# An inner Strassen level, in place, for a second product of the output stage

## The chip, the cores and the metric

The kernel runs on one core of a Trainium2 chip. The metric is device time in microseconds (us) of that core for one execution. Median before: 909.28 us over 3 runs (909.12 to 909.48).

## The reference, cut to what matters

The depth is 1, so that only the pooling mixer runs: a norm of the rows, an input product of 1024 x 2048, trailing means over windows of 2, 4, 8 and 16 rows in four channel groups, a map for each group, a gate, an output product of 1024 x 1024, the residual, and a last norm of the rows.

```
h = x                                            # 4096 x 1024, float32
u, gate = split(rms_norm(h, norm_w) @ in_w, 2)
pooled  = trailing_mean(u per group, window) - u
y       = (pooled @ group_w + group_b) * scale * silu(gate)
h       = h + y @ out_w
out     = rms_norm(h, final_norm_w)
```

## The kernel before, in words

**Stages.** `steps` lists the work in order: stage "a" and stage "b" (each half of the channel groups, 4 blocks of 1024 rows, with the group maps folded into the input weights), then stage "o", the output product, 8 blocks b of 512 rows (`NBO`, `TO`). Every block's product is done by the Strassen-Winograd scheme: seven products P1 to P7 of half-size operands, in stage "o" in the order of `ORDER_OUT`: P1, P7, P6, P2, P5, P4, P3.

**Float32 by three passes.** An operand is kept as a high part (a copy that is rounded, on ScalarE) and a low part (operand minus high part, on VectorE); `split` makes both, in one of four tiles `op0` to `op3` that are used in turn (`next_op`). A product adds high x high, high x low and low x high (`mm3`). A product of stage "o" is 2 row groups j x 4 k x 3 passes, that is 24 matmuls of 128 columns of weights against 512.

**Banks.** PSUM has 8 banks, in pairs. `sets_of` gives each block of stage "o" a pair x (P1, then P2 on top), a pair v (P7, then P4 on top), a pair y (P1 copied in by ScalarE, then P6, P5 and P3 on top) and a spare pair; the next block turns the roles by three pairs, so that the old spare pair is the new x, the old x the new v, and the old v the new y. `evict_o` takes each product from its pair: P7, P6 and P2 are copied by ScalarE into rows `hs[b]` in SBUF (and `add_h` has GpSimd issue transfers that add x to them), P5, P4 and P3 are added to these rows by VectorE (line 1245). A row is done after P4 (the lower half of the block, half 1) or P3 (the upper half, half 0); `finish` then takes the sum of squares on ScalarE (line 1121, the squares themselves thrown into a free SBUF tile), works out 1/rms in `inverse` with a square root on ScalarE and small steps on VectorE and GpSimd, scales the rows on VectorE (line 1125) and stores them by SP.

**Inner products.** From block 2 on, P2 is itself done by seven inner products ("leaves") of quarter-size operands (`split_inner`, `product_inner`, line 879): 7 x 2 k x 3 passes, that is 42 matmuls against 256 columns. Their results lie in x and in the spare pair and are put together by adds on VectorE (`add_inner`, line 889). The inner weights of P2 are formed during block 1 (`load_inner`, `form_inner`) and lie in four tiles that are taken out of the pool for good (`kept`). In stage "b", blocks 1 and 2, product P7 is done by 14 leaves in place (`product_seven`, line 725): the results move between the halves of one bank pair by copies on ScalarE (`move`), later leaves add on top, and one add on VectorE ends it.

**What sets the order.** The functions issue the instructions; a scheduler orders each engine's queue at build time, held by the explicit `issue_after` edges, and each engine works its queue strictly in that order. `advance` runs ahead of the products: loads by 4 steps, splits by 2. `split_o` forms the operands of stage "o" (s3 = s11 - s21 for P7, and so on) from four loaded quarters of y, s11, s12, s21 and s22. Tiles come from two pools, `st` (11) and `vt` (8); `take` gives the one that has been free the longest, and a load into it waits for that tile's last reader or transfer. All loads and stores of this stage wait in SP's one queue.

Of the kernel before, what the change touches and what calls it, by code (L numbers as in the profile page):

```python
# [25 lines left out]
HIST = 16  # L26
NS = 11
NV = 8
EPS = 1e-6

P1, P2, P3, P4, P5, P6, P7 = range(1, 8)
# [33 lines left out]
def kernel(  # L65
# [739 lines left out]

    inner, inner_w, kept = {}, {}, []
# [5 lines left out]
    def load_inner():  # L814
        inner_w["raw"] = [take() for _ in range(2)]
        for h, u in enumerate(inner_w["raw"]):
            nc.sync.dma_start(out=u, in_=wod[P2][h])

    def form_inner(stage):

        pattern, sizes = "p (n k s a) -> p n k s a", dict(n=2, k=2, s=2)
        if stage == 0:
            us = inner_w.pop("raw")
            b11, b12 = (quarter(us[0], j) for j in range(2))
            b21, b22 = (quarter(us[1], j) for j in range(2))
            raw = inner_w["sums"] = [take(pattern, **sizes) for _ in range(2)]
            (t3, t2), (t1, t4) = ([r[:, n] for n in range(2)] for r in raw)
            sub(t3, b22, b12)
            add(t2, t3, b11)
            sub(t1, b22, t2)  # L830
            sub(t4, b21, t2)
            for u in us:
                give(u)
            return
        r = inner_w["sums"][stage - 1]
        hi, lo = (
            kept.pop().rearrange("p x (y s a) -> p x y s a", y=2, s=2) for _ in range(2)
        )
        copy(hi, r)
        sub(lo, r, hi.bitcast(F32))  # L840
        give(r)
        for n, i in enumerate(((P7, P6), (P5, P4))[stage - 1]):
            inner_w[i] = [v[:, n] for v in (hi, lo)]
        for i, (h, j) in {P1: (0, 0), P2: (1, 0), P3: (1, 1)}.items():
            inner_w[i] = [quarter(w[P2][h][:, s], j) for s in range(2)]

    def split_inner(u):

        at = u.rearrange("p (g k) (j c) -> p g j k c", g=2, j=2)
        a11, a21, a12, a22 = (at[:, g, j] for g in range(2) for j in range(2))  # L850
        v = take("p (n k c) -> p n k c", n=4, k=2)
        sub(v[:, 0], a11, a21)
        sub(v[:, 1], a22, v[:, 0])
        add(v[:, 2], v[:, 1], a11)
        sub(v[:, 3], a12, v[:, 1])
        ts = [
            next_op("p (s g k j c) -> p s g j k c", s=2, g=2, k=2, j=2),
            next_op("p (s n k c) -> p s n k c", s=2, n=4, k=2),
        ]
        split(ts[0].rearrange("p s g j k c -> p s (g k) (j c)"), u)  # L860
        split(ts[1], v)
        give(v)
        t = {P1: ts[0][:, :, 0, 0], P2: ts[0][:, :, 1, 0], P4: ts[0][:, :, 1, 1]}
        t.update({i: ts[1][:, :, n] for n, i in enumerate((P7, P6, P5, P3))})
        return t

    def product_inner(i):

        t, sets = inner["t"], inner["sets"]
# [4 lines left out]
        for k in range(2):  # L874
            a = [t[i][:, s, k] for s in range(2)]
            b = [inner_w[i][s][:, k].rearrange("p s a -> p a s") for s in range(2)]
            ps = bank.rearrange("p (a s) -> p a s", s=2)[:, half * P : (half + 1) * P]
            for n, (x1, x2) in enumerate(((a[0], b[0]), (a[0], b[1]), (a[1], b[0]))):
                latest[0] = nc.tensor.matmul(  # L879
                    ps, x1, x2, start=i in (P1, P7) and k + n == 0, stop=k == 1 and n == 2,  # L880
                    skip_group_check=True,
                ).ins

    def add_inner(bank, *places):

# [5 lines left out]
    def sets_bank(n):  # L891
        return inner["sets"]["spare"][n]

    def product_out(i, t, sets, last):
        ps = sets[bank_of[i]]
        if isinstance(t, dict):
            inner.update(t=t, sets=sets)
            for p in (P2, P3, P4, P1, P7):
                product_inner(p)
            return  # L900
        for j in range(2):
            if j == 1 and inner and i == P5:
                product_inner(P6)
                add_inner(0, (1, 0))
                add_inner(1, (1, 0), (1, 1))
            rows = slice(j * P, (j + 1) * P)
            size = H // 4 if last and j == 1 else H // 2
            for c in range(0, H // 2, size):
                dst = sets["spare"][0] if c else ps[j]
                for k in range(4):  # L910
                    wk = w[i][k // 2]
                    mm3(
                        dst,
                        (t[:, 0, k, rows], t[:, 1, k, rows]),
                        (wk[:, 0, k % 2], wk[:, 1, k % 2]),
                        (i in (P1, P7) or c > 0) and k == 0,
                        k == 3,
                        slice(c, c + size),
                    )

# [147 lines left out]
    def load_o(b, i):  # L1068
        s = oxs[b]
        if i == P1:  # L1070
            s["11"] = load_y(b, 0, 0)
        elif i == P7:
            s["21"] = load_y(b, 1, 0)
        elif i == P6:
            s["22"] = load_y(b, 1, 1)
        elif i == P2:
            s["12"] = load_y(b, 0, 1)
            load_h(b, 1)
        elif i == P5:
            load_h(b, 0)  # L1080

    def split_o(b, i):
        s = oxs[b]
        if i == P2 and b > 1:
            return split_inner(s["12"])
        t = next_op("p (s a b) -> p s a b", s=2, a=4)
        if i == P7:
            s["3"] = take("p (a b) -> p a b", a=4)
            sub(s["3"], s["11"], s["21"])
        elif i == P6:  # L1090
# [22 lines left out]
        r = b * TO + (1 - half) * TH + j * P  # L1113
        return slice(r, r + P)

    def finish(b, half):
        ss = small.tile([P, 2], F32, tag="ss", name=f"oss{b}_{half}")
        us = [hs[b].pop((half, j)) for j in range(2)]
        for j in range(2):
            junk = take("p (a b) -> p a b", a=2)  # L1120
            nc.scalar.activation(junk, us[j], AF.Square, accum_out=ss[:, j : j + 1])
            give(junk)
        rs = inverse(b, half, ss)
        for j in range(2):
            nc.vector.scalar_tensor_tensor(  # L1125
                out=us[j], in0=us[j], scalar=rs[:, j : j + 1], in1=fw[0],
                op0=ALU.mult, op1=ALU.mult,
            )
            nc.sync.dma_start(
                out=out[row_of(b, half, j), :], in_=us[j].rearrange("p a b -> p (a b)")  # L1130
            )
            give(us[j])
# [81 lines left out]
    def evict_o(b, i, sets):  # L1214
# [64 lines left out]
        if final and i == P5:  # L1279
            for j in range(2):  # L1280
                early_half(half, j, n)
        elif not final and i in (P4, P3):
            finish(b, 1 if i == P4 else 0)

# [37 lines left out]
    def run(n, between=None, behind=None, seeds=4):  # L1322
        kind, b, i = steps[n]
        sets = sets_of(kind, b)
        if kind == "o":
            product_out(i, split_up.pop(n), sets, n == len(steps) - 1)
            evict_o(b, i, sets)
        else:
# [231 lines left out]
        )  # L1560

    scales, summed = {}, []
    stages = (P6, P5, P4)
    forming_seven = (P7, P6, P5, P4)

    for n in range(2, len(steps)):
# [4 lines left out]
        if ahead:  # L1571
# [12 lines left out]
        if kind == "o" and b == 1 and len(kept) < 4 and not inner_w:  # L1584
            while len(kept) < 4 and len(st.free) > 2:
                kept.append(st.keep())
            if len(kept) == 4:
                load_inner()
        elif kept:
            keep[0] = 0  # L1590
        advance("split", n, split_step, split_reach)
        if kind == "o" and b == 1 and i in stages:
            with tc.issue_after(latest_split[0]), tc.issue_after(latest_copy[0]):
                form_inner(stages.index(i))
# [105 lines left out]
```

## Time and profile before

| | |
|---|---|
| median of 3 runs | 909.28 us |
| profiled execution | 909.13 us, span 907.3 us, granted clock 0.997 |
| PE busy | 898.9 us (99%) |
| PEld busy | 790.2 us (87%) |
| DVE busy | 731.5 us (81%) |
| ACT busy | 494.0 us (54%) |
| POOL busy | 83.9 us (9%) |

PE is TensorE with its matmuls, PEld its weight loads, DVE VectorE, ACT ScalarE, POOL GpSimd, and SP the queue that issues most transfers. The page has the busy time of each engine, the chain of work that ended last, the costliest groups of instructions, and the transfers. The other views used here are the timeline (start, length, engine, line, what was written from what, and in square brackets how long the engine had been idle and who ended it), groups of instructions by shape (busy time, mean ns of one), busy time by stretches, waits, and transfers with the time from issue to landing. Lengths on one engine overlap a little: the next instruction can start some 0.08 us before the end of the one before. Matmul ends are modelled.

### The profile page before, as it was taken

The numbers are of one execution on the slowest core, as the hardware profiler recorded it, in microseconds if no ns is written. First come the engines' busy times: TensorE is split into PE (matmuls) and PEld (weight loads), VectorE is DVE, ScalarE is ACT, GpSimd is POOL, SyncE is SP. The second block draws the span as 40 slices with busy tenths as digits, with TensorE's granted clock in tenths as the row PEclk, the third lists the DMA queues.
The fourth block names the chain that finished last, engine by engine and source line by source line (L and its number), as shares of the span: only waits on it lengthen the run. The fifth ranks groups of instructions, "written<-read, shape, count | busy, mean of one in ns | idle before, by whom it ended". The sixth has DMA issues, their size and how long they took to land.

```text
span 907.3 us, 11824 instructions
## 1 busy us (share of the span) xinstructions
PE 898.9 (99%) x4392; PEld 790.2 (87%) x4392; DVE 731.5 (81%) x868; ACT 494.0 (54%) x760; POOL 83.9 (9%) x166
## 2 busy tenths in 40 slices
PE   9999999999999999999999999999999999999996
PEld 7888888888888888889889888888888898988986
DVE  3889896985995999798599499599759768868686
ACT  7869547447446565346545636545535435445434
POOL 0020100100110000000000000001122113112200
PEclk9999999999999999999999999999999999999998
DMA  9987667677575462323554475528585675775732
GB/s 341 401 303 238 251 229 229 215 270 251 224 267 198 161 217 85 110 100 116 206 189 148 176 267 168 192 70 232 173 232 172 171 192 158 169 220 162 175 140 92
DMA packets 71401, 179.41 MB, mean 198 GB/s; under 512 B 6576, under 2 KB 24624, under 8 KB 71344
## 3 DMA queue, kind: packets, MB, share of 16 engines
q1 hardware_dynamic: 58720, 146.13, 46.4%
q0 software_dynamic: 11904, 31.48, 13.5%
q10 hardware_dynamic: 720, 1.06, 0.3%
q8 instruction: 34, 0.56, 0.3%
q14 instruction: 23, 0.19, 0.1%
HBM read 117.81 MB, written 60.83 MB: 197 GB/s over the span
## 4 chain that ended last, share of the span: by engine, by line
PE 95%; DVE 2%; DMA 1%; ACT 1%; issue 0%; DVEq 0%; ACTq 0%
PE bank L779 89%; PE bank L879 3%; PE bank L725 2%; PE bank L421 1%; DMA st<-in_x 1%; DMA early<-in_wut 0%; ACT st L461 0%; DVE vt L1245 0%; ACT st L1152 0%; PE bank L487 0%; DVE vt L172 0%; DVE w L169 0%; ACT st L443 0%; ACT early L443 0%; DVE vt L1204 0%
## 5 line engine op out<-in xcount | busy, mean ns | idle before, releaser
L779 PE MATMUL bank<-op,w 128*128 128x512 f32 x2592 | 560.9, 379 | 0.0
L779 PEld LDWEIGHTS bank<-op,w 128*128 128x128 f32 x2592 | 489.4, 189 | 70.2 <-ACT vt L175 0.4
L779 PE MATMUL bank<-w,op 128*128 128x512 f32 (+1 forms) x1212 | 262.2, 377 | 0.0
L779 PEld LDWEIGHTS bank<-w,op 128*128 128x128 f32 x1212 | 226.0, 189 | 31.0
L169 DVE TENSOR_TENSOR op<-st,op 128x1024 fp32r<-128x1024 f32 x134 | 162.3, 1219 | 58.0 <-ACT op L175 57.6
L175 ACT ACTIVATE op<-st 128x1024 fp32r<-128x1024 f32 x134 | 140.2, 1052 | 113.4 <-PE bank L779 64.5
L175 ACT ACTIVATE vt<-bank 128x512 f32<-128x512 f32 (+1 forms) x115 | 65.8, 590 | 46.5 <-PE bank L779 43.1
L169 DVE TENSOR_TENSOR st<-st,st 128x1024 f32<-128x1024 f32 (+1 forms) x42 | 45.8, 1104 | 18.9 <-ACT st L256 16.8
L169 DVE TENSOR_TENSOR op<-vt,op 128x1024 fp32r<-128x1024 f32 x42 | 51.1, 1219 | 8.1 <-ACT op L175 8.1
L175 ACT ACTIVATE op<-vt 128x1024 fp32r<-128x1024 f32 x42 | 44.1, 1054 | 24.9 <-PE bank L779 20.9
L1062 POOL DMA_DIRECT2D st<-in_x x19 | 16.8, 893 | 387.0 <-DVE op L169 352.9
L175 ACT ACTIVATE st<-bank 128x512 f32<-128x512 f32 (+1 forms) x61 | 34.7, 585 | 30.6 <-PE bank L779 19.1
L175 ACT ACTIVATE bank<-bank 128x512 f32<-128x512 f32 (+1 forms) x60 | 32.1, 537 | 30.1 <-PE bank L779 26.0
L933 DVE TENSOR_TENSOR_SCAN vt<-vt,window 128x1040 f32<-128x1040 f32 x16 | 37.9, 2376 | 1.6 <-DMA yd<-vt 1.5
L169 DVE TENSOR_TENSOR w<-st,w 128x1024 fp32r<-128x1024 f32 (+1 forms) x26 | 30.8, 1198 | 9.2 <-ACT w L175 9.2
L175 ACT ACTIVATE w<-st 128x1024 fp32r<-128x1024 f32 (+1 forms) x26 | 26.6, 1035 | 17.4 <-PE bank L779 9.5
L175 ACT ACTIVATE vt<-tails 128x32 f32<-128x32 f32 x28 | 6.3, 228 | 46.8 <-DVE vt L933 25.7
L979 DVE SCALAR_TENSOR_TENSOR vt<-vt,vt 128x1024 f32<-128x1024 f32 x24 | 29.3, 1219 | 0.3
L172 DVE TENSOR_TENSOR st<-st,vt 128x1024 f32<-128x1024 f32 x22 | 26.1, 1215 | 3.4 <-DMA vt<-rd 3.4
L1125 DVE SCALAR_TENSOR_TENSOR vt<-vt,ors,st 128x1024 f32<-128x1024 f32 x18 | 22.5, 1282 | 7.6 <-POOL ors L235 7.6
L1245 DVE TENSOR_TENSOR st<-bank,st 128x512 f32<-128x512 f32 x23 | 15.8, 689 | 14.0 <-PE bank L779 14.0
L984 DVE SCALAR_TENSOR_TENSOR st<-vt,colt,st 128x512 f32<-128x512 f32 x38 | 26.8, 743 | 0.1
(143 smaller groups left out, 735.3 us busy)
## 6 DMA issues: line engine op xcount, KB each, us to landing
st<-in_xt SPq DMA_DIRECT2D x28, 512.0 KB, 6.3
sd<-st POOLq DMA_DIRECT2D x28, 512.0 KB, 4.0
st<-sd SPq DMA_DIRECT2D x26, 512.0 KB, 4.2
st<-in_x SPq DMA_DIRECT2D x20, 512.0 KB, 6.0
st<-yd SPq DMA_DIRECT2D x20, 512.0 KB, 4.6
yd<-st SPq DMA_DIRECT2D x19, 512.0 KB, 3.1
out<-vt SPq DMA_DIRECT2D x18, 512.0 KB, 4.6
st<-wod SPq DMA_DIRECT2D x15, 512.0 KB, 4.0
```

What stands on the lines that cost most here:

```text
L169: return nc.vector.tensor_tensor(out=dst, in0=a, in1=b, op=ALU.subtract)
L172: nc.vector.tensor_tensor(out=dst, in0=a, in1=b, op=ALU.mult)
L175: return nc.scalar.activation(dst, src, func)
L725: latest[0] = nc.tensor.matmul(cell(n, c).rearrange("p (a s) -> p a s", s=2), x1, x2, start=i == P1 and k + m == 0, stop=k == 1 and m == 2 ...
L779: latest[0] = nc.tensor.matmul(ps, a, b, start=start and n == 0, stop=stop and n == 2, skip_group_check=True).ins
L879: latest[0] = nc.tensor.matmul(ps, x1, x2, start=i in (P1, P7) and k + n == 0, stop=k == 1 and n == 2, skip_group_check=True,).ins
L933: nc.vector.tensor_tensor_scan(out=sums_[:, HIST:], data0=flat[:, HIST:], data1=flat[:, HIST - win : 2 * end - win], initial=first_sum, op ...
L979: nc.vector.scalar_tensor_tensor(out=s[:, :, at : at + H], in0=s[:, :, at : at + H], scalar=1.0 / win, in1=v[:, :, HIST:], op0=ALU.mult, o ...
L984: nc.vector.scalar_tensor_tensor(out=sg[:, j], in0=s[:, j, at : at + H], scalar=bias_c[2 * grp + j], in1=sg[:, j], op0=ALU.add, op1=ALU.mult,)
L1062: nc.gpsimd.dma_start(out=hs[b][half, j][:, n], in_=x[row_of(b, half, j), n * H : (n + 1) * H], accum_op=ALU.add,)
L1125: nc.vector.scalar_tensor_tensor(out=us[j], in0=us[j], scalar=rs[:, j : j + 1], in1=fw[0], op0=ALU.mult, op1=ALU.mult,)
L1245: partial["added"] = nc.vector.tensor_tensor(out=dst, in0=src, in1=dst, op=ALU.add).ins
```

## The change

- **P7 of blocks 3 to 7** (`OWN = 3`) is done by seven leaves in place. The pair v holds four cells of 256 columns. Leaf P1 goes to cell 1 and P5 to cell 3; ScalarE copies cell 1 to cell 0 and cell 3 to SBUF (`m5`); P2 is added to cell 0, P6 to cell 1; cell 1 is copied to cell 2; P7 is added to cell 2, P3 to cell 1; cell 2 is copied to cell 3; P4 is added to cell 2; at last VectorE adds `m5` to the whole second bank. The first two leaves run inside outer P1, ahead of its last six matmuls, and the first twelve matmuls of outer P6 fill the gaps behind the copies (`own_first`, `own_rest`, `piece`).
- **Operands**: `split_own` forms four inner sums of s3 on VectorE and splits s3 and the sums, so P7 takes two op tiles instead of one. The inner weights of P7 are formed in block 2, those of P2 still in block 1, now in the place of the loaded tiles and partly over weights that are done with; six tiles instead of four leave the pool.
- **P2**: the leaves run in the order P2, P4, P1, P3, P7, and the inner sums are split later (`late_split`), behind the last of the copies.
- **finish**: each row's squares are two instructions of 512 elements that write into idle PSUM banks (v or y of the block); the two partial sums are added on GpSimd, and the square root on ScalarE waits for that. From block 2 on the scaling of the lower rows comes behind the inner sums of the next block (`late_rows`).
- **load_h**: the rows' tiles are taken when P1 (lower half) and P2 (upper half) of their own block run, no longer ahead with the loads (but for the last block).

The diff, cut to its core:

```
+    def split_own(u):
+        ...
+        sub(v[:, 0], b12, b11)
+        sub(v[:, 1], b22, v[:, 0])
+        sub(v[:, 2], b22, b12)
+        row_sums[0] = sub(v[:, 3], b21, v[:, 1]).ins
+        plain_op = next_op("p (s g k j c) -> p s g j k c", s=2, g=2, k=2, j=2)
+        split(plain_op.rearrange("p s g j k c -> p s (g k) (j c)"), u)
+        sums_op = next_op("p (s n k c) -> p s n k c", s=2, n=4, k=2)
+        split(sums_op, v)
+    def own_move(dst, src):
+        with tc.issue_after(own.get("moved", latest_copy[0])):
+            own["moved"] = copy(own["m5"] if dst is None else own_cell(dst), own_cell(src)).ins
+    def own_first(t, b, sets):
+        own_into(P1, 1, True)
+        own_into(P5, 3)
+        ...
+        own_move(0, 1)
+        own_move(None, 3)
+    def own_rest(piece):
+        own_into(P2, 0)
+        own_into(P6, 1)
+        own_move(2, 1)
+        piece(0)
+        own_into(P7, 2)
+        own_into(P3, 1)
+        own_move(3, 2)
+        piece(1)
+        own_into(P4, 2)
+        bank = own["v"][1].rearrange("p (j b) -> p j b", j=2)
+        add(bank, bank, own["m5"].unsqueeze(1).to_broadcast([P, 2, 256]))
...
-            for p in (P2, P3, P4, P1, P7):
+            for p in (P2, P4, P1, P3, P7):
...
-    def finish(b, half):
+    def finish(b, half, sets):
+        parts = small.tile([P, 2, 2], F32, tag="parts", name=f"parts{b}_{half}")
...
-            junk = take("p (a b) -> p a b", a=2)
-            nc.scalar.activation(junk, us[j], AF.Square, accum_out=ss[:, j : j + 1])
-            give(junk)
+            for n in range(2):
+                nc.scalar.activation(
+                    sets["v" if half else "y"][j], us[j][:, n], AF.Square,
+                    accum_out=parts[:, n, j : j + 1],
+                )
+        nc.gpsimd.tensor_tensor(out=ss, in0=parts[:, 0], in1=parts[:, 1], op=ALU.add)
         rs = inverse(b, half, ss)
+        if half and b + 1 >= OWN:
+            late_rows.append(lambda: norm_rows(b, half, us, rs))
+        else:
+            norm_rows(b, half, us, rs)
...
+        if kind == "o" and b >= OWN and i == P1:
+            t = split_up.pop(n)
+            out_part(P1, t, sets["x"][0], 0, range(4))
+            out_part(P1, t, sets["x"][1], 1, range(2))
+            own_first(split_up.pop(n + 1), b, sets)
+            with tc.issue_after(latest[0]):
+                out_part(P1, t, sets["x"][1], 1, range(2, 4))
+            evict_o(b, i, sets)
+        elif kind == "o" and b >= OWN and i == P7:
+            def piece(m):
+                with tc.issue_after(latest[0]):
+                    out_part(P6, split_up[n + 1], sets["y"][0], 0, range(2 * m, 2 * m + 2))
+            own_rest(piece)
+            evict_o(b, i, sets)
...
+        (2, P1): lambda: load_inner(P7),
+        (2, P6): lambda: sum_inner(P7),
+        (2, P5): lambda: split_weight(P7, P7, P6),
+        (2, P4): lambda: (split_weight(P7, P5, P3), end_weights(P7)),
```

More of the change, by code (lines that the diff above doesn't have):

```diff
@@ L804, in product_in @@
             between[8]()
-    inner, inner_w, kept = {}, {}, []
+    inner, inner_w, kept, gathered = {}, {}, [], []
     def quarter(u, j):
         return u.rearrange("p k (s a) -> p k s a", s=2)[:, :, :, j * P : (j + 1) * P]
[L814 to L845, printed above, removed]
@@ new lines, with leaf @@
+    own = {}
+    def leaf(t, ws, i, bank, half, start=False):
+        ps = bank.rearrange("p (a s) -> p a s", s=2)[:, half * P : (half + 1) * P]
+        with tc.issue_after(latest[0]):
+            for k in range(2):
+                a = [o[:, k] for o in t[i]]
+                b = [o[:, k].rearrange("p s a -> p a s") for o in ws[i]]
+                for n, (x1, x2) in enumerate(((a[0], b[0]), (a[0], b[1]), (a[1], b[0]))):
+                    latest[0] = nc.tensor.matmul(
+                        ps, x1, x2, start=start and k + n == 0, stop=k == 1 and n == 2,
+                        skip_group_check=True,
+                    ).ins
@@ L873, in product_inner @@
         }.get(i, (sets["spare"][0], 0))
[L874 to L882, printed above, removed]
+        leaf(inner["t"], inner_w, i, bank, half, i in (P1, P7))
     def add_inner(bank, *places):
@@ L909, in product_out @@
                 dst = sets["spare"][0] if c else ps[j]
[L910 to L919, printed above, removed]
+                out_part(i, t, dst, j, range(4), slice(c, c + size), c > 0)
     def window_sums(s, v, win):
@@ L1077, in load_o @@
             s["12"] = load_y(b, 0, 1)
-            load_h(b, 1)
-        elif i == P5:
+            if b == NBO - 1:
+                load_h(b, 1)
+        elif i == P5 and b == NBO - 1:
             load_h(b, 0)
@@ L1282, in evict_o @@
         elif not final and i in (P4, P3):
-            finish(b, 1 if i == P4 else 0)
+            finish(b, 1 if i == P4 else 0, sets)
     steps = [("a", b, i) for b in range(NB) for i in ORDER_IN]
```

149 lines of the change are left out of this document (127 added, 22 removed).

## The prediction

> **What bounds the kernel now.** First the page: the busy times, then the chain that ended last.
>
> ```profile
> span 907.3 us, 11824 instructions
> ...
> PE 898.9 (99%) x4392; PEld 790.2 (87%) x4392; DVE 731.5 (81%) x868; ACT 494.0 (54%) x760; POOL 83.9 (9%) x166
> ...
> PE 95%; DVE 2%; DMA 1%; ACT 1%; issue 0%; DVEq 0%; ACTq 0%
> ```
>
> PE is the bound nearly everywhere: a matmul less is time less, and any work on VectorE or ScalarE is free until PE waits for it. Next PE's timeline in the output stage.
>
> ```profile
> 772.56 1.50 PE L879 MATMUL bank<-w,op 128*128 128x256 f32 x12
> 773.90 0.83 PE L879 MATMUL bank<-inner,op 128*128 128x256 f32 x6
> ...
> 782.43 26.07 PE L779 MATMUL bank<-w,op 128*128 128x512 f32 x120
> 808.33 1.50 PE L879 MATMUL bank<-w,op 128*128 128x256 f32 x12
> ```
>
> From start to start, 120 matmuls of 512 columns take 808.33 - 782.43 = 25.90 us, 0.2158 each; 12 of 256 take 773.90 - 772.56 = 1.34, 0.1117 each. A block lasts 808.33 - 772.56 = 35.77, which is 144 x 0.2158 + 42 x 0.1117: no gap is left. The other engines, over four such blocks:
>
> ```profile
> sum 143.08, PE 143.08 PEld 127.63 DVE 106.94 ACT 70.52 POOL 32.59; mean PE 35.77 PEld 31.91 DVE 26.74 ACT 17.63 POOL 8.15
> ```
>
> VectorE is busy 26.7 us of a block's 35.8. It is in the cover that a change can break.
>
> **What the change removes.** In each of blocks 3 to 7, P7 goes from 24 x 0.2158 = 5.18 us to 42 x 0.1117 = 4.69. That is 0.49 us, 2.45 in five blocks. Leaves in place exist already, in stage "b":
>
> ```profile
> 417.38 2.84 PE L725 MATMUL bank<-op,w 128*128 128x256 f32 x24
> ...
> 426.98 62.33 PE L779 MATMUL bank<-op,w 128*128 128x512 f32 x288
> ```
>
> 84 leaves took 9.60 us there against 84 x 0.1117 = 9.38, so copies between leaves cost 0.11 for a product at most, when the cover holds. I take 2.45 (1.9 with that cost). Outside these blocks PE's list has the same counts, so nothing more is gained: the first bound of the range is 909.28 - 2.45 = 906.8. The profiled execution took 909.13 for its span of 907.3; 1.83 lies outside the span and stays, and the median is 0.15 above it. I count from the median. A difference of 0.2% (1.8 us) is what I call measurable here.
>
> **What it adds.** Durations:
>
> ```profile
> L169 DVE TENSOR_TENSOR op<-st,op 128x1024 fp32r<-128x1024 f32 x44 | 53.3, 1218 | 19.1 <-ACT op L175 19.0
> L175 ACT ACTIVATE op<-st 128x1024 fp32r<-128x1024 f32 x43 | 45.1, 1056 | 64.5 <-PE bank L779 40.5 <-DVE st L169 10.8 <-PE bank L879 7.8
> L1125 DVE SCALAR_TENSOR_TENSOR vt<-vt,ors,st 128x1024 f32<-128x1024 f32 x18 | 22.5, 1282 | 7.6 <-POOL ors L235 7.6
> ...
> L1245 DVE TENSOR_TENSOR vt<-bank,vt 128x512 f32<-128x512 f32 x30 | 20.4, 683 | 5.7 <-PE bank L779 5.6
> ...
> L175 ACT ACTIVATE vt<-bank 128x512 f32<-128x512 f32 x27 | 15.8, 591 | 6.2 <-PE bank L779 5.8
> ...
> L889 DVE TENSOR_TENSOR vt<-bank,vt 128x256 f32<-128x256 f32 x36 | 14.1, 420 | 1.9 <-PE bank L879 1.8
> ...
> L216 ACT ACTIVATE otmp<-oss,eps 128x2 f32<-128x2 f32 x14 | 4.1, 290 | 0.8
> L1152 ACT ACTIVATE st<-vt 128x512 f32<-128x512 f32 x5 | 3.2, 632 | 9.1 <-DVE vt L889 7.0 <-DVE vt L1245 2.0
> ```
>
> And from the two seven-leaf products in stage "b", a copy between cells and the closing add:
>
> ```profile
> 423.00 0.37 ACT L175 ACTIVATE bank<-bank 128x256 f32<-128x256 f32 x1
> ```
>
> ```profile
> 425.13 0.70 DVE L762 TENSOR_TENSOR bank<-bank,st 128x512 f32<-128x512 f32 x1 [0.89 <-PE bank L725]
> ```
>
> The turn of a block on VectorE, before:
>
> ```profile
> 755.42 0.16 DVE L220 RECIPROCAL ors<-otmp 128x2 f32<-128x2 f32 x1
> 755.50 0.67 DVE L1245 TENSOR_TENSOR vt<-bank,vt 128x512 f32<-128x512 f32 x1
> 756.78 1.28 DVE L1125 SCALAR_TENSOR_TENSOR st<-st,ors,st 128x1024 f32<-128x1024 f32 x1 [0.62 <-POOL ors L235]
> 757.99 1.28 DVE L1125 SCALAR_TENSOR_TENSOR vt<-vt,ors,st 128x1024 f32<-128x1024 f32 x1
> 759.18 0.68 DVE L1245 TENSOR_TENSOR vt<-bank,vt 128x512 f32<-128x512 f32 x1
> 759.78 1.22 DVE L169 TENSOR_TENSOR st<-vt,st 128x1024 f32<-128x1024 f32 x1
> 760.92 0.42 DVE L169 TENSOR_TENSOR st<-vt 128x256 f32<-128x256 f32 x1
> ```
>
> Back to back, a 1024-wide operation takes 1.14 us (759.78 to 760.92), and by the same overlap of 0.08 a 256-wide one about 0.36 (0.42 in the row), an add from PSUM 0.60. VectorE gains in each of the five blocks one low part (1.14), four sums (4 x 0.36 = 1.4) and the closing add (0.6): 3.2, so about 30 of 35.3 us. ScalarE gains one copy (1.06), four moves (1.5) and 8 squares of 0.63 for 4 of 1.06 (about 1): 21 of 35.3. Neither becomes the bound by its sum; the place in the queue decides.
>
> *The first wait: the copy to cell 0.* Set T = 0 at a block's first matmul. The first leaf ends after 18 outer matmuls and 6 inner, 3.88 + 0.67 = 4.55; the second at 5.22; six more outer ones end at 6.52, and then leaf P2 needs cell 0 copied. On ScalarE that copy stands behind the end of the previous block: two squares for each upper row, the square root, and now a GpSimd add between them. The last row is added up by VectorE (line 1245 above); call E the end of that add. Then come two squares with their sums (2 x 0.63 + 0.1), P1's copy of 0.55 in whose shadow GpSimd adds, the root 0.29 and the copy 0.37; some 0.15 goes on hand-overs. PE can go on at E + 2.7, so E may be 3.8. Before, this block's first matmul starts at 782.43 + 48 x 0.2158 - 35.77 = 757.02, and E is 759.18 + 0.68 - 757.02 = 2.8. One us is in hand. Behind the copy on ScalarE stand P1's second copy, which P6's second bank wants at 11.8, and P2's high part, whose low part is wanted at 15.1; both have 3 us and more.
>
> Now I follow VectorE's queue through block 4. The closing add waits for the last leaf, 24 + 12 matmuls and 7 leaves after T = 0, and starts at 12.66 (36 x 0.2158 + 42 x 0.1117, and 0.2 that I allow for a hand-over from PE). ScalarE's copy of P7's second row waits for it (13.4), two more copies follow (0.55 each), then P5's high part at 15.1 and its low part on VectorE at 16.2 to 17.4. VectorE stood idle for 1.8. The tile that this low part reads last receives the next block's s21, and that load takes
>
> ```profile
> st<-yd SPq DMA_DIRECT2D x6, 512.0 KB, 4.5
> ```
>
> from issue to landing: 22.0. The next block's s3 waits for it on VectorE, and ahead of the adds of P5. From there it works without a break: six wide operations (6.8), six 256-wide (2.2), five adds of inner results (2.0), five of rows (3.0), two scalings (2.5), waits on ScalarE and GpSimd for about 1.3, and the last add, 0.7: E = 22.0 + 18.5 - 35.3 = 5.2, a stall of 1.4 to 1.6 at block 5. By the same count, block 2 (inner weights of P7 formed there, 8 operations of 0.6 more, and the same kind of load landing at 17.5) ends with E = 5.0, and there P1's copy stands between the squares, which adds 0.5: a stall of 1.6 at block 3. Block 3 gives E = 4.2, a stall of 0.4. Blocks 5 and 6 have the load out of this place, E = 2.6 and 3.5: none. Sum 3.5, between 0 (E at most 3.8, as before the change) and 6 (each of these loads 1 us later).
>
> *The second wait: s21 of block 6.* It goes into the tile of block 4's upper row, which must first be scaled and stored. In SP's queue stand two loads of x ahead of it, themselves behind stores. In block 5 the square root ends at E + 2.1 = 7.3, then 1.36 to the first scaling (755.42 to 756.78), 1.28, and the store:
>
> ```profile
> L1129 SPq DMA_DIRECT2D out<-vt x9: 332/351/382, 721.3 to 829.0; - x9
> ...
> DMA to landing us min/median/max: 2.7/5.1/8.6
> ```
>
> The view by tile gives 2.7 to 8.6 us to landing, 5.1 in the middle. 7.3 + 1.4 + 1.3 + 5.1 + 4.5 = 19.6, then s3 (1.2) and, next in VectorE's queue, the low part of block 5's P5 (1.2): 22.0. PE wants it after 48 matmuls and 12 leaves, 18.4, or 20.0 with the stall above. Wait 2.0; 0 to 5 by the store's 2.7 and 8.6.
>
> *At nothing:* the new order of P2's leaves and the later split (ready at 14.4, wanted at 17.1); the scalings behind the sums and the squares in PSUM (they take SBUF tiles out of the way, and PE waited for neither); six kept tiles (their price is the loads above); the end of the last block, whose products behind P7 are unchanged.
>
> Sum: -2.45 + 3.5 + 2.0 = +3.05; forecast **912.3 us**.
>
> **Rivals.** *Faster.* VectorE catches up, and all waits stay inside PE's cover: 906.8 to 907.4. It speaks for it that PE has no gap before and 1 us is in hand at each turn, and that my walk adds hand-overs up. It decides itself at E below 3.8 and loads that land within 3 us. *Same.* One of the waits comes, the other not, or both at half their price: -2.45 + 3.5 = +1.05, 910.3; 907.5 to 911.1. *Slower by more.* The GpSimd steps, now in ScalarE's way, get long:
>
> ```profile
> L217 POOL TENSOR_SCALAR oms<-oss x14: 182/263/1172, 646.4 to 867.4; 128x2 f32<-128x2 f32 x14
> ```
>
> If the new add takes 1.17 instead of 0.26 each time, E may only be 2.9: about 0.9 more at blocks 3, 4, 5, 0.6 at block 7 and 0.9 in the second wait, 4.2 together: 916.5. The median row speaks against its happening each time. The Trainium skill, GPSIMD Engine Reference, section Specifications, says that GpSimd's SBUF interfaces are shared with VectorE, with contention beside VectorE instructions of two SBUF inputs. By that rule, the new add would often be slow, as VectorE does little else; the spread of that row agrees with it, without showing the cause.
>
> **How the numbers follow.** Forecast (911.1 to 915) 0.38, slower by more 0.10, same 0.25, faster 0.27. Slower is thus 0.48. Leaving out the tail above 916.0 and what lies below 906.7, the range is 906.7 to 916.0; that of the likeliest case alone 911.1 to 915.
>
> **What would show it.** Right: PE gaps of over 1 us ahead of the third leaf in blocks 3 and 5, released by ScalarE's copy; a gap ahead of P5 in block 5, released by VectorE; block 6 at 35.3. Wrong: block times of 35.3 throughout, E below 3.8 at all turns, or gaps elsewhere: at P7's leaf behind the second copy, or at P6.

## The result and the profile after

The changed kernel took 933.92 us in the median (931.56 to 937.52, 4 runs) against 909.38 us (909.12 to 910.97, 4 runs) of the kernel before on the same chip: a ratio of 1.0270, 95% interval 1.0233 to 1.0306. The forecast of 912.3 us (906.7 to 916.0) had the sign and missed the size: 24.5 us more, not 3.

From the page of the changed kernel (its profiled execution took 937.52 us, the longest of the four):

```profile
span 935.7 us, 12163 instructions
...
PE 905.3 (97%) x4482; PEld 795.2 (85%) x4482; DVE 751.7 (80%) x908; ACT 513.6 (55%) x847; POOL 82.5 (9%) x180
...
PE 76%; DVE 8%; DMA 6%; issue 5%; ACT 4%; POOL 1%; SPq 0%; DVEq 0%; POOLq 0%; ACTq 0%
```

The chain that ended last ran for 95% of its time on PE before; now 19% of it are VectorE, transfers and issue. The waits of PE name whom it waits for (total, times, longest):

```profile
PE bank L920 <- DVE vt L979: 15.8, 4, 7.0
PE bank L920 <- DVE st L979: 2.9, 1, 2.9
PE bank L780 <- ACT st L176: 1.8, 1, 1.8
PE bank L780 <- DVE op L170: 0.9, 1, 0.9
...
PE bank L920 <- ACT bank L176: 0.6, 1, 0.6
```

Line 979 is `add_inner` (line 889 before): VectorE's adds of P2's inner results. P2's leaves P6 and P5 go into the bank that these adds still have to read, so PE cannot go on without them. 18.7 us of waits stand there, once in each of blocks 2 to 6 (below, blocks 2, 5 and 6; blocks 3 and 4 follow), in a place that the forecast never looked at.

```profile
714.27 1.65 PE L920 MATMUL bank<-inner,op 128*128 128x256 f32 x6 [4.98 <-DVE vt L979]
...
837.52 1.65 PE L920 MATMUL bank<-inner,op 128*128 128x256 f32 x6 [6.98 <-DVE vt L979]
...
880.58 0.94 PE L920 MATMUL bank<-w,op 128*128 128x256 f32 x6 [2.85 <-DVE st L979]
```

The forecast's own two waits are the last two rows, 0.6 and 0.9 us. (The 1.8 us lie at 222 us, before the output stage.)

What holds these adds up is seen in VectorE's timeline of block 5:

```profile
825.70 1.23 DVE L170 TENSOR_TENSOR vt<-vt,vt 128x1024 f32<-128x1024 f32 x1 [3.37 <-DMA vt<-yd]
...
832.50 1.23 DVE L167 TENSOR_TENSOR vt<-vt,vt 128x1024 f32<-128x1024 f32 x1 [4.44 <-issue]
...
837.05 0.42 DVE L979 TENSOR_TENSOR vt<-bank,vt 128x256 f32<-128x256 f32 x1
```

The first row is the next block's s3, the second its s21 + s22, both of which need loads of y; the add for PE comes after them in the same queue. For the second row the view names no releaser, but the load that it needs, issued at 822.7, took 9.8 us to land, which is 832.5. In the kernel before, the three stand in the same order, and VectorE goes from one to the next without such a wait:

```profile
770.87 1.23 DVE L169 TENSOR_TENSOR st<-vt,st 128x1024 f32<-128x1024 f32 x1
...
773.14 1.22 DVE L166 TENSOR_TENSOR st<-st,st 128x1024 f32<-128x1024 f32 x1
...
775.51 0.42 DVE L889 TENSOR_TENSOR vt<-bank,vt 128x256 f32<-128x256 f32 x1
```

In block 2 of the changed kernel the chain shows the whole of it:

```profile
701.37 8.99 DMA st<-yd
...
713.88 0.35 DVE vt L979
...
714.27 1.65 PE bank L920 x6
```

In blocks 2 to 5 (15.8 us) a load of y is what holds up the adds. In block 6 (2.9 us) it is another transfer: the add of P5's rows, ahead of them in the queue, waits for `add_h`'s transfer of x.

```profile
879.50 0.69 DVE L1358 TENSOR_TENSOR vt<-bank,vt 128x512 f32<-128x512 f32 x1 [3.97 <-DMA vt<-in_x]
```

PE's timeline shows the waits of blocks 3 and 4, and what they leave behind:

```profile
757.58 0.94 PE L920 MATMUL bank<-w,op 128*128 128x256 f32 x6 [2.43 <-DVE vt L979]
758.35 16.10 PE L780 MATMUL bank<-w,op 128*128 128x512 f32 x66
...
796.21 0.94 PE L920 MATMUL bank<-w,op 128*128 128x256 f32 x6 [1.39 <-DVE vt L979]
796.98 14.41 PE L780 MATMUL bank<-w,op 128*128 128x512 f32 x66
```

The same 66 matmuls take 1.69 us more behind a gap of 2.43 us than behind one of 1.39. The view by stretches (length, busy us of PE, PEld, DVE, ACT, POOL, then granted clock, DMA share, GB/s) has the reason in its granted clock, 0.50 against 1.00:

```profile
759.00:761.00 2.00, 2.00 (x6) 1.59 (x5) 2.00 (x5) 0.50 (x1) 0.91 (x2) 0.50 0.00 0
...
798.00:800.00 2.00, 2.00 (x11) 1.74 (x10) 2.00 (x5) 0.13 (x1) 0.00 (x0) 1.00 0.00 0
```

The account of this execution closes to 0.6 us: waits of PE in the output stage 15.8 + 2.9 + 0.9 + 0.6 = 20.2; the 1.8 before it, which nothing here explains; and 8.3 put down to matmuls at half clock, as PE was busy for 905.3 us here and for 897.0 with the same 4482 matmuls and no such gap (the last experiment). That is 30.3, against 935.7 - 907.3 = 28.4 and the 2.45 gained, 30.85.

### The profile page after: what moved, and what is told of

Its sections match the earlier page's. It is cut to its first block, busy times and chain, and to the rows that moved or that the text cites. A ratio compares the mean times of both kernels' runs of the same rounds, so it can differ in the third digit from the quotient of the medians.

```text
span 935.7 us, 12163 instructions
## 1 busy us (share of the span) xinstructions
PE 905.3 (97%) x4482; PEld 795.2 (85%) x4482; DVE 751.7 (80%) x908; ACT 513.6 (55%) x847; POOL 82.5 (9%) x180
## 4 chain that ended last, share of the span: by engine, by line
PE 76%; DVE 8%; DMA 6%; issue 5%; ACT 4%; POOL 1%; SPq 0%; DVEq 0%; POOLq 0%; ACTq 0%
PE bank L780 70%; DMA st<-yd 3%; PE bank L726 2%; DVE op L170 2%; PE bank L920 2%; DMA vt<-in_x 1%; PE bank L422 1%; DVE vt L1358 1%; ACT op L176 1%; ACT bank L1225 1%; DMA early<-in_wut 1%; DMA st<-wvd 1%; DVE vt L1238 1%; DVE vt L170 1%; DMA vt<-yd 1%
## 5 line engine op out<-in xcount | busy, mean ns | idle before, releaser
L780 PE MATMUL bank<-w,op 128*128 128x512 f32 (+1 forms) x1092 | 244.9, 382 | 0.9 <-DVE op L170 0.9
L780 PEld LDWEIGHTS bank<-w,op 128*128 128x128 f32 x1092 | 205.5, 193 | 29.4 <-DVE op L170 1.3
L170 DVE TENSOR_TENSOR op<-st,op 128x1024 fp32r<-128x1024 f32 x125 | 151.5, 1220 | 44.8 <-ACT op L176 44.4
L176 ACT ACTIVATE op<-vt 128x1024 fp32r<-128x1024 f32 x56 | 58.5, 1052 | 69.8 <-PE bank L780 53.9
L170 DVE TENSOR_TENSOR op<-vt,op 128x1024 fp32r<-128x1024 f32 x56 | 67.9, 1219 | 11.1 <-ACT op L176 11.0
L1156 POOL DMA_DIRECT2D vt<-in_x x31 | 28.3, 1014 | 444.2 <-DVE vt L1027 352.9
L170 DVE TENSOR_TENSOR st<-st,st 128x1024 f32<-128x1024 f32 (+1 forms) x37 | 42.9, 1174 | 19.6 <-ACT st L257 16.8
L1225 ACT ACTIVATE bank<-vt 128x512 f32<-128x512 f32 x42 | 25.2, 600 | 36.3 <-DVE vt L1358 35.7
L920 PEld LDWEIGHTS bank<-w,op 128*128 128x128 f32 x264 | 33.7, 191 | 10.4 <-DVE vt L979 4.6
L920 PE MATMUL bank<-w,op 128*128 128x256 f32 x264 | 35.3, 277 | 7.3 <-DVE vt L979 3.8
L920 PE MATMUL bank<-inner,op 128*128 128x256 f32 x198 | 28.4, 286 | 12.0 <-DVE vt L979 12.0
L920 PEld LDWEIGHTS bank<-inner,op 128*128 128x128 f32 x198 | 26.2, 200 | 13.7 <-DVE vt L979 13.2
```

Of the source, the lines that this page charges most:

```text
L170: return nc.vector.tensor_tensor(out=dst, in0=a, in1=b, op=ALU.subtract)
L176: return nc.scalar.activation(dst, src, func)
L780: latest[0] = nc.tensor.matmul(ps, a, b, start=start and n == 0, stop=stop and n == 2, skip_group_check=True).ins
L920: latest[0] = nc.tensor.matmul(ps, x1, x2, start=start and k + n == 0, stop=k == 1 and n == 2, skip_group_check=True,).ins
L1156: nc.gpsimd.dma_start(out=hs[b][half, j][:, n], in_=x[row_of(b, half, j), n * H : (n + 1) * H], accum_op=ALU.add,)
L1225: nc.scalar.activation(sets["v" if half else "y"][j], us[j][:, n], AF.Square, accum_out=parts[:, n, j : j + 1],)
```

## The experiments

All ratios are to the kernel before in the same comparison. A tile rotates when loads and operands take it in turn: 14 of the 19 do in the kernel before (four hold inner weights, one the weights of the final norm), 12 in the changed kernel.

| kernel | tiles that rotate | median us | ratio (95%) |
|---|---|---|---|
| changed | 12 | 933.92 | 1.0270 (1.0233 to 1.0306) |
| no leaves in place | 12 | 944.14 | 1.0384 (1.0368 to 1.0399) |
| no leaves, 3 kept tiles | 15 | 909.66 | 1.0001 (0.9991 to 1.0010) |
| the same, 1 tile unused | 14 | 913.71 | 1.0046 (1.0028 to 1.0064) |
| the same, 2 unused | 13 | 928.76 | 1.0212 (1.0194 to 1.0229) |
| the same, 3 unused | 12 | 942.38 | 1.0358 (1.0329 to 1.0388) |
| changed, s3 behind the adds | 12 | 921.10 | 1.0132 (1.0104 to 1.0159) |
| and P5's rows behind them | 12 | 936.02 | 1.0280 (1.0256 to 1.0305) |
| and late squares | 12 | 932.03 | 1.0247 (1.0229 to 1.0265) |
| s3, P5's rows, sums in place | 12 and a sum tile | 930.81 | 1.0234 (1.0213 to 1.0255) |
| all four | 12 and a sum tile | 934.14 | 1.0270 (1.0254 to 1.0286) |
| s3 behind the adds, plain x | 12 | 915.10 | 1.0061 (1.0045 to 1.0078) |
| and late squares | 12 | 915.90 | 1.0076 (1.0063 to 1.0090) |
| and sums in place | 12 and a sum tile | 916.84 | 1.0085 (1.0071 to 1.0099) |
| sums in place, early squares | 12 and a sum tile | 912.99 | 1.0043 (1.0030 to 1.0055) |
| and late root | 12 and a sum tile | 909.32 | 0.9996 (0.9987 to 1.0005) |
| and last rows late | 12 and a sum tile | 907.79 | 0.9982 (0.9973 to 0.9991) |

Theory A: PE waits for the adds of inner results, these stand behind s3 and s21 + s22 in VectorE's queue, and those wait for loads that start late because fewer tiles rotate.

**No leaves in place.**

```
-OWN = 3
+OWN = 8
```

> The changed kernel with P7 of every block as two full products again; the six kept tiles, the weights formed for P7's inner products, the loads, the squares in PSUM and P2's new order stay. Theory A (PE waits for the adds of P2's inner results, which stand in VectorE's queue behind the next block's s3 and s21 + s22, and these wait for loads that start late because only 12 tiles rotate): the in-place products play no part, so the gaps ahead of the inner products of P5 and P6 stay; 915 to 932 us. Theory B (the in-place products' own copies, sums and splits load ScalarE and VectorE too heavily): the loss goes with them; 909 to 911 us, no gap ahead of P5's and P6's inner products.

Here a quarter of P7's full weights has been overwritten by the inner weights that are still formed, so the values of P7 are others. It took 944.14 us, more than the changed kernel and more than either theory gave. B is out: the loss is there without a single leaf in place. PE waits in the same place:

```profile
PE bank L920 <- DVE vt L979: 25.1, 4, 8.5
```

**No leaves, three kept tiles; then the tiles alone.** The first drops the forming of P7's weights and the three tiles for it; the others keep one, two or three tiles more from block 2 on and leave them unused.

```
-            while len(gathered) < 3 * min(b, 2) and ...
+            while len(gathered) < 3 * min(b, 1) + K * (b > 1) and ...     # K = 0, 1, 2, 3
-        (2, P1): lambda: load_inner(P7),          # and the three lines behind it
```

> As the run without in-place products, and also without the weights formed for P7, so that three tiles are kept and not six (15 rotate, 12 before this edit). Loads, squares in PSUM, late rows and P2's order stay as changed. Theory A (too few tiles make the loads late): 908.5 to 912 us, y loads land before they are wanted, no gap ahead of P5's and P6's inner products. Theory C (the other edits, the later loads of x, the squares in PSUM with GpSimd's add, or P2's order, cost the time): above 915 us. Theory B: 909 to 911 us, as without in-place products.

> Dose of tiles alone, 1 of 3: the kernel without in-place products and without the weights formed for P7 (909.7 us with 3 kept tiles), with one tile more kept from block 2 on and left unused: 14 rotate. Theory A (the tile count makes loads late, and late loads stop VectorE ahead of the adds that PE waits for): 909 to 915 us. A theory in which the forming of P7's weights costs the time: 909 to 911 us at every dose.

> The same with two tiles kept unused: 13 rotate. Theory A: between the dose of one and that of three, 915 to 930 us. Forming theory: 909 to 911 us.

> The same with three tiles kept unused: 12 rotate, as in the changed kernel, with no product in place and nothing formed for P7. Theory A: 935 to 948 us, as the run without in-place products (944.1), with gaps of 5 to 8 us ahead of P6's inner product once in a block. Forming theory: 909 to 911 us.

909.66, 913.71, 928.76, 942.38 us: all in the ranges of A, though the gaps with three unused tiles spread wider than expected (0.8 to 6.8 us, twice in block 2) and one of 1.3 us is left in block 2 with none unused. Three tiles that nobody uses cost 32.7 us; from the 14 of the kernel before to 12 it is 28.7. With 15 tiles the other edits (P2's order, the loads of x, squares in PSUM) cost nothing; with 14, as many as before, the kernel is 4 us slower than the kernel before, so at an equal number of tiles they are not shown to be free. The forming theory is out too. How tiles become time shows in SP's, PE's and VectorE's timelines. With no tile unused, the last two loads that s3 and s21 + s22 need are issued 12.2 and 10.3 us before P2's first leaf at 811.20, and VectorE has s3 done in time (its wait is put down to a store, not to a load of y):

```profile
799.01 0.38 SPq L1139 DMA_DIRECT2D vt<-yd  x1
800.95 0.38 SPq L1139 DMA_DIRECT2D st<-yd  x1
```

```profile
811.20 0.83 PE L920 MATMUL bank<-w,op 128*128 128x256 f32 x6
```

```profile
808.41 1.23 DVE L170 TENSOR_TENSOR st<-vt,st 128x1024 f32<-128x1024 f32 x1 [2.58 <-DMA out<-st]
...
815.93 0.42 DVE L979 TENSOR_TENSOR st<-bank,st 128x256 f32<-128x256 f32 x1
```

With three unused, three loads go out together, 5.3 us or less before that leaf (at 825.62), and the queue order, which is nearly the same, now matters:

```profile
820.29 0.38 SPq L1139 DMA_DIRECT2D vt<-yd  x1
820.76 1.64 SPq L1139 DMA_DIRECT2D st<-yd  x2
```

```profile
828.64 1.23 DVE L170 TENSOR_TENSOR vt<-st,st 128x1024 f32<-128x1024 f32 x1 [5.90 <-DMA st<-yd]
834.15 1.23 DVE L167 TENSOR_TENSOR st<-st,st 128x1024 f32<-128x1024 f32 x1 [4.28 <-DMA st<-yd]
...
837.56 0.42 DVE L979 TENSOR_TENSOR vt<-bank,vt 128x256 f32<-128x256 f32 x1
```

**s3 behind the adds.** `inner_last` is the last add of `add_inner`. PE's list is the same as in the changed kernel.

```
-            split_up[n] = split_o(b, i)
+            with tc.issue_after(inner_last[0]) if i in (P7, P6) and inner_last[0] else nullcontext():
+                split_up[n] = split_o(b, i)
```

> The changed kernel with one thing more: the next block's s3 and s21 + s22 (and what is split from them) are issued behind the last add of P2's inner results of the block before. PE's own list is the same. Theory A: the waits of PE on the adds of inner results go, in blocks 2 to 5 at least (16 of their 17 us, with the stretches at half clock behind them); block 6, whose add waited for a transfer of x, may keep its 2.9. Result 907 to 915 us. Theory B (VectorE and ScalarE have too much to do): the work is the same and only its order differs, so the time stays above 925 us, with the gaps elsewhere.

921.10 us: the order alone gives back 12.8 us, about half, above what A had expected. No wait of PE behind a load of y is left; the three largest of those that remain are of other kinds:

```profile
730.71 0.94 PE L920 MATMUL bank<-w,op 128*128 128x256 f32 x6 [2.31 <-ACT bank L176]
...
825.10 0.94 PE L920 MATMUL bank<-w,op 128*128 128x256 f32 x6 [2.08 <-DVE st L979]
...
865.86 1.65 PE L920 MATMUL bank<-w,op 128*128 128x256 f32 x6 [4.30 <-DVE st L979]
```

The first is the forecast's first wait, in block 3. In the other two the adds stand behind P5's row add, which waits for `add_h`'s transfer of x onto P7's rows. It starts late, because P7's last leaf is now spread over P6, and meets three loads of y:

```profile
864.79 0.69 DVE L1358 TENSOR_TENSOR vt<-bank,vt 128x512 f32<-128x512 f32 x1 [7.55 <-DMA vt<-in_x]
```

**P5's rows behind the adds, late squares, sums in place, all four.**

```
+            with tc.issue_after(behind):                 # P5's two row adds; behind = inner_last[0]
+                nc.vector.tensor_tensor(out=u, in0=plain(ps[j]), in1=u, op=ALU.add)
...
+        own_move(0, 1)
+        with tc.issue_after(own["moved"]):
+            late_finish.pop()()                          # late squares: the last rows' finish
...                                                       # the lower rows' tiles are taken behind it too
...
+        split(plain_op..., u)                            # sums in place, in split_own
+        sub(b12, b12, b11); sub(b22, b22, b12); sub(b11, b22, b11); sub(b21, b21, b22)
+        split(sums_op..., u)
```

> The kernel with s3 and s21 + s22 behind the inner adds, and now also P5's two row adds behind them, so that VectorE's wait for the transfers that add x to P7's rows no longer holds up PE. Theory A (all that is left in blocks 5 and 6 is this wait): the gaps of 2.1 and 4.3 us ahead of P5's and P6's inner products go with the 1.7 us or so at half clock behind each: 910 to 914 us, PE waiting for ScalarE's copy to cell 0 alone (4 us). Rival D (the transfer is late for everything: s3, P4's rows and the end of the block are stuck behind it just as well): 917 to 922 us, with longer waits at the copy to cell 0 or at P3's banks.

> The same, and the squares of a block's last rows stand behind the next block's copy to cell 0 on ScalarE, not ahead of it. Theory A (the first wait of the forecast is real once the others are out of the way): the 4 us of waits on ScalarE's copy go, 1.7 us more where the gap of 2.3 was followed by half clock: 905 to 910 us. Rival E (later squares make the scalings, stores and loads late): no faster than without this edit, with the gaps at P5's and P6's inner products or at P7's second row back.

> The kernel with rows and order moved, and the four sums of s3 formed in place, behind the split of s3 itself, so that one tile more rotates. Theory A (tiles make the loads late): the median y load is issued earlier, the transfers of x meet fewer loads, and the time is 1 to 4 us below the same kernel with sums in a tile of their own. Rival F (the sums now wait for the split, and the second leaf is late): gaps ahead of the second in-place leaf, 1 to 5 us above.

> All four edits: s3 and s21 + s22 behind the inner adds, P5's rows behind them, squares behind the copy to cell 0, sums in place. If the waits named are all there are, the forecast's first bound is reached: 906.5 to 909 us. If the rivals E or F hold, 910 to 918 us.

All four missed, at 931 to 936 us. With P5's rows moved, no leaf of P2 waits for the adds any more, yet each of five blocks has two other gaps, a new one at P6's operand and the one at the copy to cell 0, grown from 4.0 to 7.8 us in all:

```profile
PE bank L780 <- DVE op L170: 9.1, 5, 2.0
PE bank L920 <- ACT bank L176: 7.8, 5, 2.5
```

The build's scheduler had rearranged the turn of the block around the new edge: s21 + s22 and P6's operand came behind the scalings, and ScalarE's copy to cell 0 behind the copy of that operand. With late squares, PE waited 1.8 us at the fourth leaf of each block, as ScalarE's copy to SBUF then stood behind the squares. With the sums in place, the four inner sums of the *next* P2 took the place ahead of the adds, again behind a load:

```profile
749.66 0.43 DVE L170 TENSOR_TENSOR st<-st 128x256 f32<-128x256 f32 x1 [6.79 <-DMA st<-yd]
```

So where the sums are in place theory A's mechanism returned with another instruction in front, and these four say nothing on rivals E and F by themselves.

**Plain x.** From the kernel with s3 behind the adds (P5's rows in their old place), x for P7's rows is loaded into the tile ahead, and P7 is added to it.

```
-            elif half == 0:
+            elif half == 0 or b >= OWN:
                 nc.sync.dma_start(out=u[:, 1], in_=x[row_of(b, half, j), H:])
...
-                copy(halved(u), plain(ps[j]))
+                add(halved(u), plain(ps[j]), halved(u)) if i == P7 and b >= OWN else copy(halved(u), plain(ps[j]))
```

> The kernel with s3 and s21 + s22 behind the inner adds (921.1 us), and x for P7's half of the upper rows loaded plainly into the tile beforehand, with P7's sums added onto it by VectorE, where they were copied by ScalarE and x added by GpSimd's transfer afterwards. Theory A (in blocks 5 and 6 VectorE's add of P5's rows waits for that transfer, and PE with it): the gaps of 2.1 and 4.3 us go, with their half clock: 909 to 914 us, waits at the copy to cell 0 (4 us) left. Rival D (two more adds on VectorE, or the plain load landing late, stop its queue instead): 918 to 926 us.

915.10 us, 1 us above A's range and below D's. The two waits for `add_h` are gone; D is out at this place. What is left is the forecast's first wait, and 1.0 us in block 7:

```profile
PE bank L920 <- ACT bank L176: 3.6, 5, 2.3
```

**Late squares and sums in place again.** Now with P1, P7, P6 and P2 of the next block all behind the adds, wherever the sums are in place; late squares stand behind both of the first copies.

> The kernel with s3 and s21 + s22 behind the inner adds and with x for P7 loaded plainly (915.1 us), and the squares of a block's last rows behind the two copies of the next block's in-place product on ScalarE. Theory A (what is left is the forecast's first wait, 3.6 us in all and 1.7 at half clock behind block 3's 2.3): these gaps go; 908.5 to 911 us. Rival E (later squares make scalings, stores and loads late): 913 us and more, with gaps at P5's and P6's inner products again.

> The same, with s3's four sums formed in place behind the split of s3, which leaves a tile more to rotate, and with all four early splits of the next block (P1, P7, P6, P2) behind the inner adds. Theory A (tiles and order decide): 907 to 910 us, loads earlier than without. Rival F (the sums stand behind the split, and the second in-place product waits for them): 912 us and more, with gaps ahead of that product.

> The sums in place and the four splits behind the inner adds, with the squares where the change has them (ahead of the copies). Theory A: 3 to 5 us above the kernel with late squares, the waits at the copy to cell 0. If the late squares cost more than they bring: below it.

915.90, 916.84 and 912.99 us: the first two miss A's ranges and lie in those of the rivals, but with gaps where no rival put them; the third is below the kernel with late squares, not 3 to 5 us above it. Late squares bring nothing: the wait moves from the copy to cell 0 to the copy between cells 1 and 2, which now stands behind the squares:

```profile
770.29 1.60 PE L920 MATMUL bank<-inner,op 128*128 128x256 f32 x12 [1.16 <-ACT bank L176]
```

With the squares early and the sums in place, 0.4 to 1.0 us a block are left at the copy to cell 0, and 1.4 in block 7. ScalarE's timeline shows that this is not work but its order: ScalarE waits for GpSimd's add, takes the root, and only then copies:

```profile
764.88 0.29 ACT L217 ACTIVATE otmp<-oss,eps 128x2 f32<-128x2 f32 x1 [0.50 <-POOL oss L1228]
765.09 0.37 ACT L176 ACTIVATE bank<-bank 128x256 f32<-128x256 f32 x1
```

**Late root, and the last rows late.** The root and the add ahead of it go behind the copies; then block 6's last scalings go behind block 7's first inner add.

```
+        own_move(0, 1)
+        own_move(None, 3)
+        with tc.issue_after(own["moved"]):
+            late_finish.pop()()                          # close_rows: GpSimd's add, root, scalings
...
+            add_inner(0, (0, 0))
+            with tc.issue_after(inner_last[0]):
+                late_norm.pop()() if late_norm else None
```

> The kernel with sums in place and the squares ahead of the copies (913.0 us); only the square root of a block's last rows, with GpSimd's add of the two parts ahead of it, now stands behind the next block's copies on ScalarE. Theory A (the rest of the first wait is the half microsecond in which ScalarE waits for GpSimd's add, and the root): the gaps of 0.4 to 1.0 us at the copy to cell 0 go, 3 us in all; 909 to 911 us, with the 1.4 us in the last block left. Rival: the wait moves to the copy between cells 1 and 2 as it did with late squares; 912 to 914 us.

> The same, and block 6's last two scalings stand behind the first add of inner results of block 7 on VectorE. Theory A (VectorE is behind by these 2.4 us in the last block, where P6's inner product waits 1.4): 1 to 1.5 us below the run without; 907 to 909.5 us, at or below the kernel before. Otherwise the same as that run.

909.32 and 907.79 us, both as A expects. The last is 0.18% below the kernel before, interval 0.09% to 0.27%: a small gain, about the size that the prediction calls measurable. Its page and PE's timeline:

```profile
PE 897.0 (99%) x4482; PEld 792.2 (87%) x4482; DVE 755.0 (83%) x916; ACT 509.2 (56%) x839; POOL 79.5 (9%) x172
```

```profile
767.12 1.50 PE L919 MATMUL bank<-inner,op 128*128 128x256 f32 x12
...
802.42 1.50 PE L919 MATMUL bank<-inner,op 128*128 128x256 f32 x12
```

A block lasts 802.42 - 767.12 = 35.30 us, against 35.77 before. VectorE does more than in the changed kernel (755.0 against 751.7 us), so the amount of its work was not the reason. PE's one wait that is left in the output stage is 0.8 us, at the copy to cell 0 in block 3.

## Why the prediction was wrong, point by point

- **The gain, 0.49 in each of five blocks, 2.45 in all: right.** 35.77 to 35.30 is 0.47, once nothing waits. The last kernel lies 1.0 us above the first bound of 906.8.
- **The step that failed: "six kept tiles (their price is the loads above)".** That price was followed to one place only, the end of the rows on VectorE (E) and the copy behind it. The text even says that s3 waits for its load on VectorE "ahead of the adds of P5", and does not ask who waits for what is queued behind s3. It is PE itself, through the adds of P2's inner results. The walk even counts "five adds of inner results" behind that load. For blocks 2 to 5 this is 15.8 us of waits that the sum has nowhere; its own two terms, 3.5 + 2.0 us, came to 1.5. The tiles alone, with no leaf in place, cost 32.7 us (12 against 15 rotating).
- **The arrival of s21: nearly right.** In block 4, whose first matmul starts at 774.29 - 18 x 0.2158 = 770.4, s3 starts at 793.20, after 22.8 us where the walk had 22.0; in block 5 (first matmul at 807.35 by the same sum) the load of s21 landed after 18.3, where the walk had 19.6. But the walk follows s21 alone. The load of s22 behind it landed after 25.2, and s21 + s22, ahead of the adds, made the longest wait of all, 6.98.
- **The load, 4.5 us from issue to landing: mis-sized.** The walk had a median of the kernel before. The load that ended the wait in block 2 took 8.99, that of s21 in block 4 took 6.9, and those of s21 and s22 in block 5 took 4.2 and 9.8. Several loads and `add_h`'s transfers were out at once; whether these stretched each other, no run takes apart.
- **`add_h` was left out of the walk.** P7's last leaf ends 12.46 us after the block's start (36 x 0.2158 + 42 x 0.1117), where P7 ended at 10.36 (48 x 0.2158), so the transfer of x can start 2 us later, and P5's row add waited for it in blocks 5 and 6 of the reordered kernel (2.1 and 4.3 us of PE); in the changed kernel it is the 2.9 us of block 6.
- **Half clock was left out**: 8.3 us, by the account above.
- **The first wait: right in kind, wrong in place.** Predicted 1.6, 0.4 and 1.5 in blocks 3, 4 and 5, 3.5 in all. In the changed kernel 0.6, in block 5 alone; PE stood still at other places in every block from 2 to 6, which may have covered the rest. Once the other waits were gone it came as 4.0 (s3 behind the adds) and 3.6 (plain x), 2.3 of it in block 3. The walk has GpSimd's add in the shadow of P1's copy; in the kernel with sums in place that copy came ahead of the last squares, and ScalarE waited 0.50 us for the add where PE waited 0.55.
- **The second wait: 0.9, not 2.0**, in the place named (block 5, ahead of P5).
- **At nothing: shown with one tile more than before only** for P2's order, late split, squares in PSUM and the loads of x (ratio 1.0001 with 15 tiles, 1.0046 with 14).
- **The rivals.** Faster and same needed the waits inside PE's cover, and this was not so. Slower by more named GpSimd's add at 1.17 us. It is short here (min/median/max in ns):

```profile
L1229 POOL TENSOR_TENSOR oss<-parts x14: 188/195/486, 648.8 to 897.3; 128x2 f32<-128x2 f32 x14
```

 The Trainium skill's rule on GpSimd's shared SBUF interfaces (GPSIMD Engine Reference, Specifications), cited there, would make this add slow beside VectorE; no trace shows that this decided anything.
- **What would show it.** The gap in block 5 ahead of P5, released by VectorE, was there. Gaps of over 1 us ahead of the third leaf were not, block 6 was not 35.3, and the gaps lay where neither list had them.

Not settled: why the changed kernel is 8 to 10 us faster than those with as few tiles and no leaf in place. Its waits are shorter above all in blocks 3 and 4 (2.4 and 1.4 us, against 8.5 and 5.8 in the first experiment). No run takes the leaves and the tiles apart in the other direction, as the leaves need the tiles.

## What to carry over

When a change takes tiles out of a rotating pool, ask of every load when its tile comes free now, which instruction waits for it, and *everything* that stands behind that instruction in its engine's queue, up to the engine that bounds the kernel. An order that was harmless while loads came early (s3 ahead of the adds, with 15 tiles as well) becomes the bound when they come late, and a new ordering edge lets the scheduler put the next early instruction into the same place: look at the whole turn again after each edge. PE's gaps cost more than their length, so one gap of 3 us is worth more effort than three of 1.

## What was not expected of the hardware

**Half clock behind short gaps.** In the 17 traces of changed kernels there are 98 waits of PE in the output stage. In the five us behind the 32 of them up to 1.11 us the granted clock stayed at 1.00; behind all 19 over 2.6 us it fell to 0.50; behind the 47 from 1.14 to 2.57 us it fell 20 times, 15 of these 20 where a second wait lay within 4.1 us. The lengths are the view's, which models the ends of matmuls. The 66 matmuls above lost 1.69 us, which gives an estimate of 3.4 us at half clock. The Trainium skill (TensorE: Matmul & The Clock Gate, "HAM oscillation — how this bites in real kernels") warns of idle gaps over about 3.4 us; the length of the slow stretch agrees with the window of that length which Part 1 of the page gives, but the gap that sets it off is shorter here: 2.43 us was enough.
